# Lending part of an activations tile to a weight stream as four more raw tiles, and moving a scratch tile of the last block

## The chip, the cores and the metric

The kernel runs on one core of a Trainium2 chip, as one program in one launch. The metric is the device time of a run in microseconds (us). The engines are named as in the profile: PE (TensorE, matmuls; PEld its weight loads), DVE (VectorE), ACT (ScalarE), POOL (GpSimd) and SP (SyncE, which here only issues DMAs).

## The reference

Two models follow one another on 256 tokens of width 1024: a block of two layers (an mLSTM mixer in layer 0, latent attention in layer 1, each followed by a mixture of experts and a gated projection) and a second block (two feed-forward layers round a retention mixer). The change touches the mixture of experts, which both layers of the first block have:

```python
def peer_ffn(x, w_q, sub_keys, u, v):            # x: 256 x 1024
    q = (xt @ w_q).reshape(T, PEER_HEADS, 2, PEER_HALF)
    s = jnp.einsum('thcd,hcnd->thcn', q, sub_keys)
    s1, i1 = lax.top_k(s[:, :, 0], K)            # K = 16, of 128 keys
    s2, i2 = lax.top_k(s[:, :, 1], K)
    cand_s = s1[..., :, None] + s2[..., None, :] # 256 candidates
    top_s, top_pos = lax.top_k(cand_s, K)
    expert_idx = ...                             # 16 of 128*128 experts per head
    gates = jax.nn.softmax(top_s, axis=-1)
    act = gelu(einsum('thkd,td->thk', u[expert_idx], x))
    out = einsum('thk,thkd->td', gates * act, v[expert_idx])
```

## The kernel before

The kernel does not gather experts. It computes x times all of u (128 blocks of 128 experts), multiplies the activations with a gate matrix that is zero wherever an expert was not chosen, and multiplies the whole with v. One tile, `big`, holds the activations: 128 partitions by 128 blocks by 256 tokens, one block being 1 KB per partition; `room(big, n)` is the stretch of blocks 4n to 4n+3, as large as one weight unit.

**Precision and the stream.** A product in float32 is made from hi and lo parts: `split` (line 439) casts a value to a shorter form, hi (on ACT, line 440), and subtracts, lo (on DVE, or POOL for some units, line 441). All weights are units of 128 x 1024 and come through one `Stream` (`Net.w`). `load` (line 261) issues each unit's DMA on SP's queue into one of three tiles `wraw`. `prep` (line 281) makes hi and lo in one of three tiles each, `whi` and `wlo`, up to three units ahead of the unit PE is at (`target`). A raw tile is free again when its lo has been made, so `load_ahead` (line 314) keeps at most three units loaded or loading beyond those prepared.

**A stage of experts** (`peer`, line 878) takes 16 query units, 128 units of u, 128 units of v, in this order. `skew` runs query units, scores and the first blocks in a staggered way. `block(b)` (line 928) does 24 matmuls of 256 columns on one unit of u (`cols_late`, line 490): 16 with hi, then 8 with lo. Beside the blocks DVE makes the selection (`select`, line 1051), given out in portions of 1.8 us per block by `spend`, and this order of DVE's is fixed by hand (`in_order`); the order on the other engines is that of a scheduler. The selection lasts until about block 41. After it the class `Gates` makes the gate matrix in steps beside the remaining blocks.

**Every third block** does not burden DVE with its lo. For units in `on_dma`, `begin` (line 293) lets ACT write x = −raw (line 298) into one of two tiles x1, taken in turn, rounded to the short form, and a POOL DMA adds the raw unit onto it, which leaves raw less its rounded form, the lo part (line 299). The lo tile of such a unit is called x in the trace. `begin` is called when the unit is the next to be prepared and has been loaded; its hi follows from `prep` (line 287).

**The end of the blocks.** `activate` (line 1035) puts the gelu of a block into `big`; for tokens whose gates are there already it goes by a scratch tile: for even blocks `gl`, for odd blocks `gates.room`, the last 1 KB of x0, a tile of `Gates`. `joins` (line 1046) multiplies it in on DVE one block later. When all blocks are done, line 965 splits the first four blocks of `big` into W[0], whose hi takes the place of x0 and is named x in the trace (its lo is another x); the following groups go to a tile named xT. Then `rows_k` (line 547) multiplies them with the units of v into four accumulators.

Of the kernel before, what the change touches and what calls it, by code (L numbers as in the profile page):

```python
# [9 lines left out]
F32 = mybir.dt.float32  # L10
F32R = mybir.dt.float32r
# [8 lines left out]
P = 128  # L20
D = 1024
S = 256
# [11 lines left out]
UNIT = 1024  # L34
# [3 lines left out]
PLE_TAIL = 5  # L38
FF_TAIL = 6
PACE = 4  # L40

GATE_SCALE = 2.0 ** 15

# [176 lines left out]
class Ring:  # L220


    def __init__(self, size, new):
        self.size, self.new, self.units = size, new, []


class Stream:
# [3 lines left out]
    def __init__(self, k, pool, tag, size, widths, src, raw=3, parts=3):  # L231
        self.pool = pool
        self.k, self.tag, self.size, self.widths, self.src = k, tag, size, widths, src
        self.n, self.i, self.loaded, self.done, self.oldest = len(widths), 0, 0, 0, 0
        self.raw, self.ahead = raw, parts
        self.raws, self.parts = {}, {}
        self.on_pool, self.on_dma = set(), set()
        self.rings = [Ring(parts, lambda i: [self.tile(i, x, F32R, parts) for x in ("hi", "lo")])]
        self.start, self.until = 0, 0
        self.begun, self.spare = {}, None  # L240

    def tile(self, i, what, dt, bufs):
        return self.pool.tile([P, self.size], dt, tag=self.tag + what, name=f"{self.tag}{what}{i}", bufs=bufs)

    def extend(self, ring, until):

        self.rings = [self.rings[0], ring]
        self.start, self.until = self.i, until
        self.tail_at(until)

    def tail_at(self, i):

        self.on_pool.update(range(i, i + 2))

    def target(self):

        if self.i < self.until:
            return min(self.i + self.ahead + min((self.i - self.start) // PACE, self.rings[1].size), self.until + self.ahead)
        return self.i + self.ahead

    def load(self, i):
        t = self.tile(i, "raw", F32, self.raw)
        w = self.widths[i]
        self.k.nc.sync.dma_start(out=t[:, :w], in_=self.src[i, :, :w])
        self.raws[i] = t

# [14 lines left out]
    def prep(self, i, ring):  # L281
        k, w = self.k, self.widths[i]
        t = self.raws.pop(i)
        ring.units.append(i)
        if i in self.begun:
            hi, lo = self.tile(i, "hi", F32R, self.ahead), self.begun.pop(i)
            k.nc.scalar.copy(hi[:, :w], t[:, :w])
        else:
            hi, lo = ring.new(i)
            k.split(t[:, :w], hi[:, :w], lo[:, :w], pool=i in self.on_pool)  # L290
        self.parts[i] = (hi[:, :w], lo[:, :w])

# [9 lines left out]
    def fill(self):  # L302
        while self.done < min(self.n, self.target()):
            ring = self.ring(self.done)
            if ring is None:
                break
            self.load_ahead()
            self.prep(self.done, ring)
            self.done += 1
        self.load_ahead()  # L310
        if self.done in self.on_dma and self.done not in self.begun:
            self.begin(self.done)

    def load_ahead(self):
        while self.loaded < min(self.n, self.done + self.raw):
            self.load(self.loaded)
            self.loaded += 1

# [27 lines left out]
class Net:  # L346
# [44 lines left out]

    def more(self, pool, tail=TAIL, until=None):

        new = lambda i: [self.t(pool, [P, UNIT], f"more{x}", F32R, bufs=tail) for x in ("hi", "lo")]
        self.w.extend(Ring(tail, new), until or self.until)

    def in_order(self):
# [70 lines left out]
    def rstd(self, pool, var, n, eps, more=None):  # L468

        t = self.t(pool, [P, n], "rstd", bufs=4)  # L470
        if more is None:
            self.nc.vector.tensor_scalar_add(t, var, float(eps))
        else:
            self.nc.vector.tensor_scalar(t, var, more, float(eps), op0=ALU.add, op1=ALU.add)  # L474
        self.nc.gpsimd.tensor_tensor(t, t, self.mhalf[:, :n], op=ALU.pow)  # L475
        return t
# [401 lines left out]
    def peer(self, layer, gain):  # L878
        nc, v, tc = self.nc, self.nc.vector, self.tc
        mm = nc.tensor.matmul  # L880
        with tc.tile_pool(name="pr", bufs=1) as pool:
            big = self.t(pool, [P, P, S], "big")
# [16 lines left out]
            steps = self.select(tk, big, ready, idx, gT, iota)  # L899

            self.w.spare = lambda n: self.t(ip if n else self.gp, [P, UNIT], "x1", F32R)
            self.w.on_dma = set(range(self.w.i + 16 + 1, self.w.i + 16 + P - 8, 3))

            sc = self.scores_of(big)
# [57 lines left out]
            gates = now["gates"]  # L962
# [12 lines left out]
            n = P // WB  # L975
# [18 lines left out]
            parts = [(W[n - 1], j) for j in range(WB)]  # L994
# [40 lines left out]
    def activate(self, big, gates, late, b, ps):  # L1035

        nc = self.nc
        t0 = gates.tokens if gates else 0
        if t0:
            y = gates.room if b % 2 else self.t(gates.pool, [P, S], "gl")  # L1040
            nc.scalar.activation(y[:, :t0], ps[:, :t0], AF.Gelu)
            late.append((big[:, b, :t0], y[:, :t0]))
        if t0 < S:
            nc.scalar.activation(big[:, b, t0:], ps[:, t0:S], AF.Gelu)
# [467 lines left out]
    def neighborhood(self, pool, y, nqk, done):  # L1512
# [83 lines left out]
        for step in range(H8 + 4):  # L1596
            for s in (3, 2, 1):
                if 0 <= step - s < H8:
                    stages[s](step - s)
            next(more)  # L1600
            next(more)
            if step < H8:
                s_scores(step)
# [22 lines left out]
class Gates:  # L1626
# [42 lines left out]
    def join(self, g, blocks, done):  # L1669

        nc, TJ = self.k.nc, self.TJ
        t = slice(g * TJ, (g + 1) * TJ)
        ps = self.ps[g].rearrange("p (t b) -> p b t", t=TJ)
        dst = self.big[:, :blocks, t] if done else self.big[:, blocks:, t]
        if done and blocks:
            nc.vector.scalar_tensor_tensor(dst, ps[:, :blocks], 1.0 / GATE_SCALE, dst, op0=ALU.mult, op1=ALU.mult)
        if not done:
            if blocks < P:
                nc.scalar.mul(dst, ps[:, blocks:], 1.0 / GATE_SCALE)
            self.tokens = (g + 1) * TJ  # L1680
            self.ps.pop(g)
# [97 lines left out]
```

## Time and profile before

| | us |
|---|---|
| timed runs | 2660.10, 2676.08, 2676.26 (median 2676.08) |
| profiled execution, its own time | 2663.04 |
| span in the profile | 2661.3 |
| PE busy | 2559.8 (96%) |
| DVE busy | 1751.7 (66%) |
| ACT busy | 1328.9 (50%) |
| POOL busy | 244.5 (9%) |
| mean granted clock of TensorE | 0.988 |

In layer 0 the query units run from about 146 to 206 us of the span, the blocks from about 206 to 642, and the units of v from 647 on; in layer 1 the blocks run from about 1202 to 1640. Times in the trace are counted from the start of the span. A row such as "5.14 <-ACT x" in brackets says how long the engine was idle ahead of an instruction and what ended it. A granted clock of 1.00 is 2.4 GHz, 0.50 is 1.2 GHz.

### The profile page before, as it was taken

The page shows a single profiled execution, that of the slowest core. Times are in us where ns is not written, and L with a number is a line of the kernel's source. Part 1 is how long each engine was busy: PE and PEld are TensorE (multiplying, and loading weights), DVE is VectorE, ACT ScalarE, POOL GpSimd, SP SyncE. Part 2 cuts the span into 40 slices and gives each one's busy share as a digit, 9 for nine tenths or more (in the row PEclk, how much of TensorE's full clock was granted, in tenths as well). Part 3 has the DMA queues.
Part 4 walks back from the last instruction along what each step waited for, and adds up shares of the span by engine and source line. Part 5 has one row for each costly group of instructions (what it writes and reads, how often), then busy time and mean ns, then how long its engine had stood idle before and what let it go on. Part 6 is the DMA issues. An engine that isn't in the chain of part 4 may idle for free. (4 is left out here: it accounts for less than half of the span.)

```text
span 2661.3 us, 42846 instructions
## 1 busy us (share of the span) xinstructions
PE 2559.8 (96%) x16706; PEld 2308.8 (87%) x16706; DVE 1751.7 (66%) x3120; ACT 1328.9 (50%) x2113; POOL 244.5 (9%) x201
## 2 busy tenths in 40 slices
PE   8999899999999998999899999999999999999998
PEld 7799899998888887899889998888887997987898
DVE  6879856677555567689856677555557546665654
ACT  5445555554444445545545554444445444554542
POOL 0560000000000003000000000000001002111000
PEclk9999999999999999999999999999999999999999
DMA  7356677776555564357677776555565654554653
GB/s 249 108 168 196 197 209 202 207 207 207 199 195 194 191 211 160 119 170 199 196 205 200 213 203 209 200 195 191 195 208 188 223 167 152 183 177 157 204 194 101
DMA packets 144620, 502.42 MB, mean 189 GB/s; under 512 B 16153, under 2 KB 22425, under 8 KB 144417
## 3 DMA queue, kind: packets, MB, share of 16 engines
q1 hardware_dynamic: 122832, 443.93, 48.3%
q0 software_dynamic: 14032, 50.86, 10.3%
q10 hardware_dynamic: 7552, 4.89, 0.6%
q8 instruction: 131, 2.15, 0.3%
q14 instruction: 73, 0.59, 0.1%
HBM read 494.38 MB, written 5.24 MB: 188 GB/s over the span
## 5 line engine op out<-in xcount | busy, mean ns | idle before, releaser
L441 DVE TENSOR_TENSOR wlo<-wraw,whi 128x1024 fp32r<-128x1024 f32 (+1 forms) x478 | 587.3, 1229 | 531.9 <-ACT whi L440 531.1
L440 ACT CAST whi<-wraw 128x1024 fp32r<-128x1024 f32 x520 | 543.8, 1047 | 599.6 <-PE acc L547 322.8
L490 PE MATMUL ub<-xT,whi 128*128 128x256 f32 x4096 | 548.5, 287 | 4.3 <-ACT whi L440 3.5
L490 PEld LDWEIGHTS ub<-xT,whi 128*128 128x128 f32 x4096 | 515.8, 194 | 7.7 <-ACT whi L440 7.2
L547 PE MATMUL acc<-whi,xT 128*128 128x512 f32 x1816 | 507.5, 392 | 12.5 <-ACT whi L440 7.2
L547 PEld LDWEIGHTS acc<-whi,xT 128*128 128x128 f32 x1816 | 341.3, 189 | 85.8 <-ACT xT L440 7.6
L441 DVE TENSOR_TENSOR morelo<-wraw,morehi 128x1024 fp32r<-128x1024 f32 (+1 forms) x214 | 261.5, 1224 | 119.4 <-ACT morehi L440 118.9
L440 ACT CAST morehi<-wraw 128x1024 fp32r<-128x1024 f32 (+1 forms) x227 | 237.1, 1047 | 188.2 <-DMA wraw<-in_wst 72.9
L547 PE MATMUL acc<-wlo,xT 128*128 128x512 f32 x908 | 282.7, 391 | 0.2 <-DVE wlo L441 0.2
L547 PE MATMUL acc<-morehi,xT 128*128 128x512 f32 x808 | 235.1, 391 | 0.2
L547 PEld LDWEIGHTS acc<-wlo,xT 128*128 128x128 f32 x908 | 171.2, 189 | 37.0 <-DVE wlo L441 1.0
L490 PE MATMUL ub<-xT,wlo 128*128 128x256 f32 x1408 | 198.1, 283 | 1.9 <-DVE wlo L441 1.7
L441 POOL TENSOR_TENSOR wlo<-wraw,whi 128x1024 fp32r<-128x1024 f32 (+1 forms) x42 | 100.8, 2403 | 1047.8 <-ACT whi L440 1042.7
L490 PEld LDWEIGHTS ub<-xT,wlo 128*128 128x128 f32 x1408 | 181.6, 192 | 3.1 <-DVE wlo L441 3.1
L547 PEld LDWEIGHTS acc<-morehi,xT 128*128 128x128 f32 x808 | 151.8, 189 | 32.3 <-ACT morehi L440 0.6
L298 ACT ACTIVATE x<-wraw 128x1024 fp32r<-128x1024 f32 x80 | 84.7, 1058 | 152.6 <-DMA wraw<-in_wst 152.6
L446 PE MATMUL ps<-xT,whi 128*128 128x256 f32 (+1 forms) x552 | 158.6, 288 | 0.0
L447 PE MATMUL ps<-xT,whi 128*128 128x256 f32 (+1 forms) x552 | 156.9, 284 | 0.4 <-DVE xT L441 0.4
L448 PE MATMUL ps<-xT,wlo 128*128 128x256 f32 (+1 forms) x552 | 156.6, 284 | 0.0
L299 POOL DMA_DIRECT2D x<-in_wst x80 | 70.0, 875 | 798.6 <-ACT x L298 245.6
L547 PE MATMUL acc<-morelo,xT 128*128 128x512 f32 x404 | 129.1, 392 | 5.0 <-DVE morelo L441 5.0
L490 PE MATMUL ub<-xT,x 128*128 128x256 f32 x640 | 95.0, 292 | 34.7 <-DMA x<-in_wst 34.6
(477 smaller groups left out, 4132.4 us busy)
## 6 DMA issues: line engine op xcount, KB each, us to landing
wraw<-in_wst SPq DMA_DIRECT2D x816, 512.0 KB, 4.0
x<-in_wst POOLq DMA_DIRECT2D x80, 512.0 KB, 5.6
wraw<-in_wst SPq DMA_DIRECT2D x10, 384.0 KB, 3.4
sp<-x SPq DMA_DIRECT2D x4, 512.0 KB, 3.0
big<-in_keys ACTq DMA_DIRECT2D x8, 256.0 KB, 6.7
sp<-big SPq DMA_DIRECT2D x4, 512.0 KB, 4.3
x<-sp POOLq DMA_DIRECT2D x4, 512.0 KB, 4.7
pp<-sp SPq DMA_DIRECT2D x4, 512.0 KB, 5.6
```

Source lines behind the costliest of these rows:

```text
L298: k.nc.scalar.mul(lo[:, :w], self.raws[i][:, :w], -1.0)
L299: k.nc.gpsimd.dma_start(out=lo[:, :w], in_=self.src[i, :, :w], accum_op=ALU.add)
L440: self.nc.scalar.copy(hi, src)
L441: (self.nc.gpsimd if pool else self.nc.vector).tensor_tensor(lo, src, hi.bitcast(F32), op=ALU.subtract)
L446: mm(ps, a[0], b[0], start=start, stop=False)
L447: mm(ps, a[0], b[1], start=False, stop=False)
L448: mm(ps, a[1], b[0], start=False, stop=stop)
L490: mm(ps[:, :S], w[of][:, k], xT[part][:, k], start=n == 0, stop=n == len(steps) - 1)
L547: mm(acc[ti][h], a, w[b][:, h * 512:(h + 1) * 512], start=first, stop=last)
```

## The change

Rooms 14 to 17 of `big` (blocks 56 to 71) hold nothing until block 56. They are lent to the stream as four more raw tiles for the first 40 units of u (`SELECT`, `LENT`), so that in this stretch seven raw tiles go round. `load_ahead` loads up to seven units beyond those prepared while units are in this range. `begin` may be called for a unit up to two units earlier than before. hi and lo tiles are taken from their ring one by one. And the scratch tiles of `activate` are exchanged: even blocks take `gates.room`, odd blocks `gl`, so that the last block, 127, does not use x0's room. The assertion in `Gates.join` guards the rooms' use.

```diff
--- before.py
+++ after.py
@@ -38,6 +38,8 @@
 PLE_TAIL = 5
 FF_TAIL = 6
 PACE = 4
+
+SELECT, LENT = 40, 4
 
 GATE_SCALE = 2.0 ** 15
 
@@ -235,9 +237,10 @@
         self.raw, self.ahead = raw, parts
         self.raws, self.parts = {}, {}
         self.on_pool, self.on_dma = set(), set()
-        self.rings = [Ring(parts, lambda i: [self.tile(i, x, F32R, parts) for x in ("hi", "lo")])]
+        self.rings = [Ring(parts, lambda i, x: self.tile(i, x, F32R, parts))]
         self.start, self.until = 0, 0
         self.begun, self.spare = {}, None
+        self.lent_raws, self.borrow = [], range(0)
 
     def tile(self, i, what, dt, bufs):
         return self.pool.tile([P, self.size], dt, tag=self.tag + what, name=f"{self.tag}{what}{i}", bufs=bufs)
@@ -248,6 +251,10 @@
         self.start, self.until = self.i, until
         self.tail_at(until)
 
+    def lend(self, raws, units):
+
+        self.lent_raws, self.borrow = raws, units
+
     def tail_at(self, i):
 
         self.on_pool.update(range(i, i + 2))
@@ -259,8 +266,8 @@
         return self.i + self.ahead
 
     def load(self, i):
-        t = self.tile(i, "raw", F32, self.raw)
-        w = self.widths[i]
+        n, w = (i - self.borrow.start) % (self.raw + len(self.lent_raws)) - self.raw, self.widths[i]
+        t = self.lent_raws[n] if i in self.borrow and n >= 0 else self.tile(i, "raw", F32, self.raw)
         self.k.nc.sync.dma_start(out=t[:, :w], in_=self.src[i, :, :w])
         self.raws[i] = t
 
@@ -282,11 +289,12 @@
         k, w = self.k, self.widths[i]
         t = self.raws.pop(i)
         ring.units.append(i)
+        hi = ring.new(i, "hi")
         if i in self.begun:
-            hi, lo = self.tile(i, "hi", F32R, self.ahead), self.begun.pop(i)
+            lo = self.begun.pop(i)
             k.nc.scalar.copy(hi[:, :w], t[:, :w])
         else:
-            hi, lo = ring.new(i)
+            lo = ring.new(i, "lo")
             k.split(t[:, :w], hi[:, :w], lo[:, :w], pool=i in self.on_pool)
         self.parts[i] = (hi[:, :w], lo[:, :w])
 
@@ -308,11 +316,12 @@
             self.prep(self.done, ring)
             self.done += 1
         self.load_ahead()
-        if self.done in self.on_dma and self.done not in self.begun:
-            self.begin(self.done)
+        for i in range(self.done, self.done + (3 if self.done + 2 in self.borrow else 1)):
+            if i in self.on_dma and i not in self.begun:
+                self.begin(i)
 
     def load_ahead(self):
-        while self.loaded < min(self.n, self.done + self.raw):
+        while self.loaded < min(self.n, self.done + self.raw + (len(self.lent_raws) if self.loaded in self.borrow else 0)):
             self.load(self.loaded)
             self.loaded += 1
 
@@ -391,7 +400,7 @@
 
     def more(self, pool, tail=TAIL, until=None):
 
-        new = lambda i: [self.t(pool, [P, UNIT], f"more{x}", F32R, bufs=tail) for x in ("hi", "lo")]
+        new = lambda i, x: self.t(pool, [P, UNIT], f"more{x}", F32R, bufs=tail)
         self.w.extend(Ring(tail, new), until or self.until)
 
     def in_order(self):
@@ -899,6 +908,9 @@
             steps = self.select(tk, big, ready, idx, gT, iota)
 
             self.w.spare = lambda n: self.t(ip if n else self.gp, [P, UNIT], "x1", F32R)
+
+            first = self.w.i + 16
+            self.w.lend([self.room(big, n) for n in range(14, 14 + LENT)], range(first, first + SELECT))
             self.w.on_dma = set(range(self.w.i + 16 + 1, self.w.i + 16 + P - 8, 3))
 
             sc = self.scores_of(big)
@@ -1037,7 +1049,7 @@
         nc = self.nc
         t0 = gates.tokens if gates else 0
         if t0:
-            y = gates.room if b % 2 else self.t(gates.pool, [P, S], "gl")
+            y = self.t(gates.pool, [P, S], "gl") if b % 2 else gates.room
             nc.scalar.activation(y[:, :t0], ps[:, :t0], AF.Gelu)
             late.append((big[:, b, :t0], y[:, :t0]))
         if t0 < S:
@@ -1675,6 +1687,7 @@
         if done and blocks:
             nc.vector.scalar_tensor_tensor(dst, ps[:, :blocks], 1.0 / GATE_SCALE, dst, op0=ALU.mult, op1=ALU.mult)
         if not done:
+            assert self.k.w.done >= self.k.w.borrow.stop
             if blocks < P:
                 nc.scalar.mul(dst, ps[:, blocks:], 1.0 / GATE_SCALE)
             self.tokens = (g + 1) * TJ
```

On ACT, in the middle of layer 0's blocks with the selection, the rows before are these (`whi_…<-wraw` is the hi of a block's unit, `x_…<-wraw` the start of a third block's lo, and `big<-ub` the gelu of a finished block):

```order
L440 CAST whi_3275<-wraw_3156 128x1024
L1044 ACTIVATE big_1652<-ub_3233 128x256
L298 ACTIVATE x_386_3281<-wraw_3197 128x1024
L287 CAST whi_3319<-wraw_3197 128x1024
L1044 ACTIVATE big_1652<-ub_3274 128x256
L1044 ACTIVATE big_1652<-ub_3318 128x256
L440 CAST whi_3358<-wraw_3238 128x1024
```

And in the change, at the same block:

```order
L295 CAST whi_3189<-big_1652 128x1024
L306 ACTIVATE x_382_3192<-wraw_3030 128x1024
L1056 ACTIVATE big_1652<-ub_3149 128x256
L449 CAST whi_3230<-big_1652 128x1024
L1056 ACTIVATE big_1652<-ub_3188 128x256
L449 CAST whi_3270<-wraw_2991 128x1024
L1056 ACTIVATE big_1652<-ub_3229 128x256
L295 CAST whi_3311<-wraw_3030 128x1024
L306 ACTIVATE x_390_3315<-big_1652 128x1024
```

Before, x and whi of one unit (`wraw_3197`) stand side by side. In the change x_382 of the raw tile `wraw_3030` stands one triple ahead of the whi_3311 of the same tile, with the gelus of two blocks and two whi between them, and the raw tiles are partly rooms of `big`.

On POOL, in layer 0 ahead of the query units (`wlo` are lo parts of query units), before:

```order
L441 TENSOR_TENSOR wlo_1719<-wraw_1512,whi_1718 128x1024
L441 TENSOR_TENSOR wlo_1765<-wraw_1597,whi_1764 128x1024
L441 TENSOR_TENSOR wlo_1818<-wraw_1603,whi_1817 128x1024
L441 TENSOR_TENSOR wlo_1871<-wraw_1722,whi_1870 128x1024
L441 TENSOR_TENSOR wlo_1924<-wraw_1768,whi_1923 128x1024
L441 TENSOR_TENSOR wlo_1976<-wraw_1821,whi_1975 128x1024
```

and in the change:

```order
L450 TENSOR_TENSOR wlo_1719<-wraw_1512,whi_1718 128x1024
L450 TENSOR_TENSOR wlo_1765<-wraw_1597,whi_1764 128x1024
L307 DMA x_339_2447<-in_wst 128x1024
L450 TENSOR_TENSOR wlo_1818<-wraw_1603,whi_1817 128x1024
L450 TENSOR_TENSOR wlo_1871<-wraw_1722,whi_1870 128x1024
L450 TENSOR_TENSOR wlo_1924<-wraw_1768,whi_1923 128x1024
```

The first DMA into an x moved ahead of eleven of these wlo; on ACT its negation moved with it. On SP the loads of the four lent rooms stand among and behind the spills of `peer` (line 1003), ahead of most of the loads of query units.

On ACT at the end of layer 0's blocks (`gl` and `x_319` are the scratch tiles, `x_683` is the hi of W[0], `xT` that of W[1], `morehi` a further unit of v), before:

```order
L1041 ACTIVATE gl_7994<-ub_7927 128x256
L440 CAST whi_8016<-wraw_7895 128x1024
L440 CAST morehi_8034<-wraw_7932 128x1024
L1041 ACTIVATE x_319_2180<-ub_7962 128x256
L440 CAST xT_8013<-big_1652 128x1024 x2
L440 CAST x_683_7997<-big_1652 128x1024
```

and in the change:

```order
L1053 ACTIVATE x_319_2180<-ub_7905 128x256
L449 CAST whi_7995<-wraw_7874 128x1024
L449 CAST x_683_7975<-big_1652 128x1024
L1053 ACTIVATE gl_7980<-ub_7941 128x256
L449 CAST xT_7992<-big_1652 128x1024 x2
L449 CAST morehi_8013<-wraw_7910 128x1024
```

x_683 moved ahead of the last gelu, of the two casts to xT and of morehi.

On DVE at the same place (`big<-gl` and `big<-x_319` are the joins, x_684 is the lo of W[0]), before:

```order
L1049 TENSOR_TENSOR big_1652<-x_319_2180,big_1652 128x256
L1049 TENSOR_TENSOR big_1652<-gl_7994,big_1652 128x256
L441 TENSOR_TENSOR wlo_8017<-wraw_7895,whi_8016 128x1024
L441 TENSOR_TENSOR morelo_8035<-wraw_7932,morehi_8034 128x1024
L1049 TENSOR_TENSOR big_1652<-x_319_2180,big_1652 128x256
L441 TENSOR_TENSOR xT_8013<-big_1652,xT_8013 128x1024 x2
L441 TENSOR_TENSOR x_684_7998<-big_1652,x_683_7997 128x1024
```

and in the change:

```order
L1061 TENSOR_TENSOR big_1652<-gl_7939,big_1652 128x256
L1061 TENSOR_TENSOR big_1652<-x_319_2180,big_1652 128x256
L450 TENSOR_TENSOR wlo_7996<-wraw_7874,whi_7995 128x1024
L450 TENSOR_TENSOR x_684_7976<-big_1652,x_683_7975 128x1024
L1061 TENSOR_TENSOR big_1652<-gl_7980,big_1652 128x256
L450 TENSOR_TENSOR xT_7992<-big_1652,xT_7992 128x1024 x2
L450 TENSOR_TENSOR morelo_8014<-wraw_7910,morehi_8013 128x1024
```

x_684 moved ahead of the last join, of xT and of morelo. The order of DVE and of PE within the blocks is the same as before but for names.

## Rows read from the trace of the kernel before

**Rows 1.** The page's costliest groups (busy us, mean ns of one | idle us before).

```profile
L298 ACT ACTIVATE x<-wraw 128x1024 fp32r<-128x1024 f32 x80 | 84.7, 1058 | 152.6 <-DMA wraw<-in_wst 152.6
...
L299 POOL DMA_DIRECT2D x<-in_wst x80 | 70.0, 875 | 798.6 <-ACT x L298 245.6
...
L490 PE MATMUL ub<-xT,x 128*128 128x256 f32 x640 | 95.0, 292 | 34.7 <-DMA x<-in_wst 34.6
```

**Rows 2.** Windows: PE, PEld, DVE, ACT, POOL busy us (instructions), granted clock, DMA share, GB/s.

```profile
206.00:294.00 88.00, 80.05 (x631) 78.51 (x630) 83.02 (x316) 41.43 (x60) 7.05 (x8) 0.96 0.69 196
294.00:348.50 54.50, 46.24 (x348) 44.84 (x348) 42.03 (x79) 31.96 (x46) 4.38 (x5) 0.94 0.70 202
642.30:656.00 13.70, 8.55 (x28) 6.50 (x28) 7.42 (x7) 5.83 (x8) 0.59 (x2) 0.75 0.48 189
1202.00:1301.00 99.00, 88.50 (x704) 86.30 (x703) 93.24 (x351) 46.60 (x68) 7.76 (x9) 0.98 0.69 197
1301.00:1343.00 42.00, 35.87 (x274) 35.45 (x273) 32.09 (x45) 26.52 (x38) 3.46 (x4) 0.92 0.68 195
1640.40:1654.00 13.60, 8.90 (x32) 6.63 (x32) 7.63 (x8) 6.34 (x8) 0.64 (x2) 0.87 0.61 203
```

**Rows 3.** DVE's waits in 207 to 293, 293 to 350 and 1300 to 1350.

```profile
DVE q L441 <- ACT q L440: 1.1, 1, 1.1
...
DVE wlo L441 <- ACT whi L440: 10.6, 6, 4.1
...
DVE wlo L441 <- ACT whi L440: 11.4, 7, 4.2
```

**Rows 4.** Waits of ACT and of SP's queue in 206 to 346.

```profile
ACT whi L440 <- DMA wraw<-in_wst: 32.8, 13, 6.0
...
SPq L264 <- DVE wlo L441: 51.5, 15, 6.3
```

**Rows 5.** PE's timeline in layer 0 (start, us, work), blocks 34 to 41.

```profile
331.55 2.08 PE L490 MATMUL ub<-xT,whi 128*128 128x256 f32 x16
...
334.43 2.08 PE L490 MATMUL ub<-xT,whi 128*128 128x256 f32 x16
...
351.36 0.49 PE L1114 MATMUL ps<-ident,big 128*128 128x128 f32 x3
351.60 0.61 PE L490 MATMUL ub<-xT,whi 128*128 128x256 f32 x3
```

**Rows 6.** PE's timeline: lo of block 27 in both layers, blocks 41 and 43 in layer 1.

```profile
300.25 1.22 PE L490 MATMUL ub<-xT,wlo 128*128 128x256 f32 x8
...
1295.04 1.21 PE L490 MATMUL ub<-xT,wlo 128*128 128x256 f32 x8 [0.20 <-DVE wlo L441]
...
1346.17 2.16 PE L490 MATMUL ub<-xT,whi 128*128 128x256 f32 x16
...
1356.21 1.22 PE L490 MATMUL ub<-xT,x 128*128 128x256 f32 x8 [2.12 <-DMA x<-in_wst]
```

**Rows 7.** Line 299, 206 to 349: issue on POOL (ns, count), and landing.

```profile
L299 POOL DMA_DIRECT2D x<-in_wst x13: 876/876/906, 210.5 to 341.7; - x13
...
DMA to landing us min/median/max: 5.3/7.1/8.4
```

**Rows 8.** POOL's timeline in layer 0's query units; ten rows like this one.

```profile
164.53 2.41 POOL L441 TENSOR_TENSOR wlo<-wraw,whi 128x1024 fp32r<-128x1024 f32 x1 [1.12 <-ACT whi L440]
```

**Rows 9.** ACT's timeline at the seam of layer 0.

```profile
641.38 1.05 ACT L440 CAST whi<-wraw 128x1024 fp32r<-128x1024 f32 x1 [1.28 <-PE ub L490]
...
646.35 1.04 ACT L440 CAST x<-big 128x1024 fp32r<-128x1024 f32 x1
```

**Rows 10.** PE at the seams of both layers: timeline, then a window of the tile acc.

```profile
647.45 1.22 PE L547 MATMUL acc<-whi,x 128*128 128x512 f32 x2 [5.14 <-ACT x L440]
...
1644.70 0.76 PE L547 MATMUL acc<-whi,x 128*128 128x512 f32 x2 [4.23 <-ACT x L440]
...
647.40:652.00 4.60, 4.55 (x10) 0.50 0.76 305
```

## The prediction

> **What bounds the kernel now.** I began with the page's costliest groups. TensorE (PE) is busy for 2559.8 of 2661.3 us, so only about 100 us can be won without taking work away, and the question is which idle stretches the change can reach. One group names a single cause: the matmuls that read the tile x (the lo part of every third block, which comes by ScalarE and a GpSimd DMA) stand idle for 34.7 us ahead of themselves, 34.6 of it until that DMA lands [rows 1].
>
> Then the busy time by stage [rows 2]. Where selection and blocks run together the loss differs from stretch to stretch: in 206 to 294 (layer 0) PE is busy for 80.05 of 88 us and VectorE (DVE) for 83.02; in 294 to 348.5 PE for 46.24 of 54.5 but DVE for only 42.03. Layer 1 has the same two phases: DVE 93.24 of 99.00 us, then 32.09 of 42. And at the seam from the blocks to the V units PE works 8.55 of 13.7 us (642.3 to 656) and 8.90 of 13.6 (1640.4 to 1654).
>
> DVE's waits tell the phases apart. In the first phase it waits for nothing but 1.1 us; in the second it waits 10.6 us in six stops in layer 0 and 11.4 in seven in layer 1, each time for ScalarE's (ACT) whi [rows 3]. So the first phase is DVE's: PE waits there for x, but it could not run ahead of the lo parts that DVE makes between steps of the selection. The second is a chain of waits round the raw tiles: ACT's whi waits 32.8 us in 13 stops for a raw tile to land, and the load on SP's queue stood 51.5 us in 15 stops behind DVE's wlo, the last reader of one of only three raw tiles [rows 4].
>
> **Selection, phase 1: nothing.** Seven raw tiles instead of three, and an x begun two units earlier, end PE's waits for x (about 7 of the 88 us). But DVE's order there is written by hand and is the same row for row, with nothing to wait for. PE's idle time moves from x to wlo. Value: 0 us. Bounds: 0, and what PE stood idle there, 88 − 80.05 = 7.95 in layer 0 and 99 − 88.50 = 10.5 in layer 1, if DVE were not the bound after all.
>
> **Selection, phase 2.** A block that waits for nothing takes 334.43 − 331.55 = 2.88 us (24 matmuls) [rows 5]. The lo matmuls of block 27 begin at 300.25 in layer 0 and at 1295.04 in layer 1 [rows 6]; I take these as set by DVE, since they close its phase. From there to the first matmul of block 41 stand 0.96 us (2.88/3, eight matmuls), 13 blocks of 2.88 = 37.44, and two groups of three transposes at 351.60 − 351.36 = 0.24, 0.5 together [rows 5]: 38.9. To this I add 1.5 for lo parts that DVE still brings late: its own work in the whole of 294 to 348.5 is 42.03 us, nearly PE's for the same blocks, so it follows closely but hardly falls behind (ends: 0, and 42.03 − 38.9 = 3.1 if DVE's work is the bound). So 40.4 us: block 41 begins at 340.7 instead of 351.60 (−10.9) and at 1335.4 instead of 1346.17 (−10.7) [rows 5, 6]. In layer 1 block 43 also waits 2.12 us for x, begun late for the same want of a raw tile [rows 6]: −2.1. Sum −23.7.
>
> Is x then early enough? In the new order ACT begins x(i+3) right behind whi(i), a whole triple of blocks ahead. Its tile comes free when PE has done block i−3, and PE wants it at the lo of block i+3: five blocks and the 16 hi matmuls of a sixth, 5 × 2.88 + 1.92 = 16.3 us. The chain is the negation, 1.06 us, the DMA's issue, 0.88, and its landing, at most 8.4 [rows 1, 7]: 10.3. There are 6 us to spare.
>
> The Trainium skill ("SBUF — State Buffer", SBUF: two separate sides) speaks against this: a DMA issued from GpSimd has its descriptors written there, and VectorE's two-port operations lock GpSimd out, so that such a DMA waits for VectorE; a denser VectorE would make x later still. By its example (about 3100 ns for 620) 2.5 us would be added and the sum would stay. Without it: the issue took 876 to 906 ns in all 13 cases between 206 and 349, with DVE at 94% in most of it [rows 2, 7], but the landing, 5.3 to 8.4 us, does spread, and I keep a later landing as a rival.
>
> **Hoisted work.** The first x of a lent tile is begun before most query units: one negation on ACT and one issue on POOL, ahead of eleven wlo that POOL makes for the query units. POOL does one in 2.41 us and then stands idle 1.12 until the next whi (ten such rows) [rows 8], so an issue of 0.9 us goes into one such gap. Value 0; 1 us per layer if it does not. SP's four early loads go past spills that nobody waits for soon: 0. The number of loads and bytes is unchanged, so are DVE's and PE's rows within the blocks.
>
> **The seam to V.** Before, ACT did whi (641.38), morehi, the last gelu, two casts to xT, and only then x, the hi of W[0], at 646.35; it could not be sooner, since the last block's gelu stood in x's room. PE stood idle 5.14 us until 647.45 [rows 9, 10]. Now x stands right behind whi. whi ends at 642.43, x at 643.48, and its lo is made behind it on DVE, after four matmuls of cover. PE last worked until 647.45 − 5.14 = 642.31, so idle is 1.2, and I add 0.3 for the lo: 1.5, a gain of 3.6. In layer 1 the idle is 4.23 [rows 10]; the same 1.5 leaves a gain of 2.7. Then the clock: after the idle stretch PE worked 647.4 to 652 at a granted 0.50 (the 1.2 GHz level), 4.55 us for what takes 2.28 at full rate [rows 10]. After the idle of 2.12 us at 1356.21, by contrast, eight matmuls took 1.22 us [rows 6], where at half clock they would take over 2 × 0.96 = 1.92; so an idle of 1.5 leaves the clock up, −2.3; in layer 1 the window's mean clock is 0.87 where layer 0's is 0.75 [rows 2], so by 0.13/0.25 about half, −1.2. Sum −9.8. Bounds: −6.3 if the clock falls all the same; 0 if x waits for something else.
>
> **Sum.** −23.7 − 9.8 = −33.5 us against the profiled execution: 2663.0 − 33.5 = 2629.5. The three timed runs and the profiled one lie at 2660.1, 2663.0, 2676.1 and 2676.3; from their middle, 2669.6, the same sum gives 2636. Between the two I say **2633 us**.
>
> **Rivals.**
> 1. *Only the seam gains* (0.13). DVE stays the bound through phase 2 as well: what it waited for before is filled by other waits of its hand-written order (the transposes and gT at the end of each half of the selection hang on PE and ACT). For it: DVE's 42.03 us are nearly PE's work. Against it: the six stops all name whi. −9.8: 2653 to 2660.
> 2. *Half of phase 2* (0.12). x lands late although it begins sooner, since seven loads in flight share the DMA engines with it and DVE is denser. Past the 6 us to spare each x stops PE again. −12 − 9.8: about 2645.
> 3. *Slower* (0.05). ACT works in order. x(i+3) now stands ahead of the gelu of block i−3 and of whi(i+1), and it waits for its raw tile and for PE to leave its own tile. Each raw load that lands late then holds up the hi parts too, which x did not before. PE has three prepared units, 3 × 2.88 = 8.6 us, less whi's 1.05 and x's 1.06 themselves: it decides from a wait of 6.5 us on. There are 2 × 13 such x; to eat the 33.5 and add 1%, 27 us, each would have to wait 6.5 + 60/26 = 8.8 us. Against it: the lent tiles are loaded seven units ahead. About 2695.
> 4. *It does not do what it says* (0.03): the lent rooms come free too late to hold loads, and all stays within 1%, 2655 to 2669.
> 5. *More* (0.10): phase 1 gains too, up to 7.95 + 10.5 of PE's idle: about 2618.
>
> **Chances and range.** The forecast itself holds 0.57: 2622 to 2645, from 0 to 3.1 us of late lo parts per layer, the clock's 3.5, and the two levels of the runs. A measurement tells about 1% from no change, here 27 us from 2676 or 2663, so a gain under 27 would be called no change: the forecast against a run of the same level is −33.5, near that bound. Faster by over 1%: 0.57 less the part in which 6 us are lost (0.09), and rivals 5 and a part of 2: 0.48 + 0.10 + 0.04 = 0.62; within 1%: 0.33; slower 0.05. For the range I take 2614, from rival 5 with the lower level, to 2657, from rival 1's lower end: it leaves out rivals 3 and 4, half of 1, and little else.
>
> **What would show it.** In phase 1 the matmuls of x no longer wait for the DMA, and those of wlo do for DVE, with DVE's waits still near nothing. The loads no longer wait for DVE's wlo, nor whi for the raw tile. From block 27 to 41 some 40 us instead of 51. x lands in 5 to 9 us but well ahead of PE. At the seams an idle of 1 to 2 us and a granted clock near 1. I am wrong if PE's idle time in phase 2 stays with another name, if ACT's x or whi waits for a raw tile for more than 6 us, or if DVE's phase 1 itself grows longer.

## The result and the profile after

| | before | after |
|---|---|---|
| median of the runs, us | 2674.40 | 2641.97 |
| runs, us | 2660.10 to 2676.26 | 2641.24 to 2642.56 |
| profiled execution, its own time, us | 2663.04 | 2641.24 |
| span of the profile, us | 2661.3 | 2639.5 |

The ratio is 0.9892, with a 95% interval of 0.9862 to 0.9922: faster by about 1.1%, 2642 us where 2633 was forecast. The kernel before has medians between 2661 and 2674 us in different series of runs, so each ratio below is against the kernel before in the same series. The two profiled executions are 21.8 us apart, and the forecast made for them was 33.5. Read off PE's matmuls in both traces, stretch by stretch:

| stretch | before, us | after, us | difference |
|---|---|---|---|
| start to block 0, layer 0 | 206.5 | 211.9 | +5.5 |
| blocks 0 to 27, layer 0 | 94.8 | 93.6 | −1.2 |
| blocks 28 to 40 | 50.3 | 38.8 | −11.5 |
| blocks 41 to 127 | 290.7 | 289.9 | −0.8 |
| idle at the seam to V | 5.14 | 1.13 | −4.0 |
| V, latent attention, query units of layer 1 | 555.0 | 561.2 | +6.2 |
| blocks 0 to 27, layer 1 | 93.6 | 93.6 | 0.0 |
| blocks 28 to 40 | 50.1 | 38.7 | −11.4 |
| blocks 41 to 127 | 294.3 | 290.8 | −3.5 |
| idle at the seam to V | 4.23 | 1.13 | −3.1 |
| from there to the end | 1016.6 | 1018.7 | +2.1 |

So the gains are where they were forecast and of about that size, and two stretches got longer: those that hold the query units. The windows of the change, in the columns of [rows 2], for the same stretches:

```profile
211.90:304.50 92.60, 83.83 (x672) 80.98 (x671) 87.65 (x333) 48.55 (x68) 7.87 (x9) 1.00 0.73 204
304.50:344.30 39.80, 39.52 (x326) 39.20 (x327) 37.83 (x63) 28.38 (x40) 3.49 (x4) 1.00 0.70 177
634.20:648.00 13.80, 12.67 (x55) 10.25 (x55) 9.77 (x10) 8.41 (x10) 2.17 (x4) 1.00 0.76 263
1196.50:1289.10 92.60, 83.88 (x673) 81.04 (x672) 87.78 (x334) 48.50 (x68) 7.74 (x9) 1.00 0.73 206
1289.10:1328.90 39.80, 39.54 (x327) 39.21 (x327) 37.80 (x63) 28.52 (x41) 3.46 (x4) 1.00 0.71 178
1619.60:1633.00 13.40, 12.27 (x53) 9.87 (x53) 9.69 (x9) 8.12 (x10) 2.01 (x4) 1.00 0.78 269
```

In the first and fourth row (blocks 0 to 27) DVE is busy for 87.65 and 87.78 of 92.6 us and PE for 83.83 and 83.88: phase 1 is DVE's as before. In the second and fifth (blocks 27 to 40) PE is busy for 39.52 and 39.54 of 39.8 us, where in [rows 2] it had 46.24 of 54.5. A part of this gain is the clock: [rows 2] have a granted 0.94 and 0.92 there, the change 1.00, which by the length of those two stretches is an estimated 3.3 us in each layer. The third and sixth rows are the seams: 12.67 of 13.8 and 12.27 of 13.4 us, and the granted clock is 1.00 instead of 0.75 and 0.87.

The page has one group that answers to the x of [rows 1]; x itself waits no longer and has left the list:

```profile
L499 PE MATMUL ub<-xT,wlo 128*128 128x256 f32 x1408 | 201.5, 286 | 18.0 <-DVE wlo L450 18.0
```

PE now stands 18.0 us for DVE's wlo. PE's waits in blocks 0 to 27 and 27 to 40 of layer 0 say where:

```profile
PE ub L499 <- DVE wlo L450: 8.0, 13, 0.9
...
PE ub L499 <- DVE wlo L450: 1.0, 2, 0.7
```

8.0 us in 13 stops in phase 1, 1.0 in phase 2. The waits of ACT and of SP's queue from 212 to 344, beside [rows 4]:

```profile
ACT x L306 <- DMA wraw<-in_wst: 4.4, 4, 1.5
ACT x L306 <- DMA big<-in_wst: 3.5, 3, 2.3
...
SPq L271 <- DVE wlo L450: 69.6, 18, 6.3
```

ACT's whi does not wait for a raw tile any more (32.8 us before); only x does, for 7.9 us in seven stops, the longest of 2.3 us, and none of them stops PE. SP's loads still wait for DVE's wlo, 69.6 us, longer than before, although the prediction had them wait no longer: with seven tiles they are that far ahead, and the wait reaches nobody.

The lo of block 27 and block 41, as in [rows 5, 6]:

```profile
304.51 1.21 PE L499 MATMUL ub<-xT,wlo 128*128 128x256 f32 x8 [0.74 <-DVE wlo L450]
...
344.07 0.49 PE L1126 MATMUL ps<-ident,big 128*128 128x128 f32 x3
344.31 1.92 PE L499 MATMUL ub<-xT,whi 128*128 128x256 f32 x14
```

From 304.51 to 344.31 are 39.8 us. Forecast were 40.4, and in the kernel before it was 51.35.

The issue and landing of x on POOL's queue, as in [rows 7]:

```profile
L307 POOL DMA_DIRECT2D x<-in_wst x14: 873/873/902, 205.5 to 340.9; - x14
...
DMA to landing us min/median/max: 5.3/6.8/9.0
```

The issue takes 873 to 902 ns with DVE at 95% in phase 1 (87.65 of 92.6 us). The Trainium skill ("SBUF — State Buffer", SBUF: two separate sides) states that a DMA issued from GpSimd has to wait while VectorE runs a two-port operation. Such a wait does not show here: the issue got no longer, the landing (5.3 to 9.0 us) only at its upper end by 0.6. No run here tells which of VectorE's operations in this stretch are of that kind.

ACT and PE at the seams, as in [rows 9, 10]: ACT in layer 0, PE in layers 0 and 1, and the window of acc behind the first.

```profile
633.29 1.05 ACT L449 CAST whi<-wraw 128x1024 fp32r<-128x1024 f32 x1 [1.48 <-PE ub L499]
634.24 1.04 ACT L449 CAST x<-big 128x1024 fp32r<-128x1024 f32 x1
...
635.34 0.73 PE L556 MATMUL acc<-whi,x 128*128 128x512 f32 x2 [1.13 <-ACT x L449]
...
1620.78 0.73 PE L556 MATMUL acc<-whi,x 128*128 128x512 f32 x2 [1.13 <-ACT x L449]
...
635.30:640.00 4.70, 4.66 (x20) 1.00 0.62 211
```

x stands right behind whi (633.29, 634.24), the idle is 1.13 us in both layers, and the clock stays at 1.00. Compared matmul by matmul the first seam brings 6.2 us (PE is ahead by 8.1 us before it and by 14.3 after it), the second 5.1.

Now what was not forecast. PE falls back by 6.3 us between 151 and 181 us of the trace of before, and by 9.4 between 1157 and 1186: at the head of the query units of both layers. SP's queue in layer 0, the change:

```profile
148.74 0.39 SPq L271 DMA_DIRECT2D big<-in_wst  x1
150.48 1.30 SPq L1015 DMA_DIRECT2D sp<-big  x2
154.28 1.11 SPq L271 DMA_DIRECT2D big<-in_wst  x2
```

Three loads of 512 KB into rooms of `big` go out between 148.74 and 155.4, among the spills. Just then ACT's queue issues the loads of the keys and, at 151.51, of iota (64 KB): one lent load goes out ahead of iota's, two within 4 us behind it. In layer 1 it is one ahead (1130.22) and three within 6 us behind (from 1135.48; iota 1132.97). In the kernel before, SP's next load goes out 5.7 us (158.21) and 4.4 us (1152.86) behind iota's. iota's landing in the change (min, median, max of the two layers):

```profile
DMA to landing us min/median/max: 11.4/13.2/15.1
```

and in the kernel before:

```profile
DMA to landing us min/median/max: 6.4/6.4/6.4
```

ACT waits for it, since the cast of iota (line 1654) stands among the first rows of the query units (layer 0, and the same row of layer 1):

```profile
162.93 0.40 ACT L1654 CAST x<-iota 128x256 f16<-128x256 f32 x1 [4.53 <-DMA iota<-in_iota]
163.24 1.05 ACT L306 ACTIVATE x<-big 128x1024 fp32r<-128x1024 f32 x1
...
1148.11 0.40 ACT L1654 CAST x<-iota 128x256 f16<-128x256 f32 x1 [8.51 <-DMA iota<-in_iota]
```

4.53 and 8.51 us, in which all that is behind it on ACT stands: the hoisted x, whi, and the q of the query units. In the kernel before ACT waited 1.4 us there in both layers together. PE's waits in the query units follow:

```profile
PE ps L455 <- ACT q L449: 2.8, 1, 2.8
...
PE ps L455 <- ACT q L449: 6.6, 1, 6.6
```

2.8 us in layer 0 and 6.6 in layer 1; before, PE waited there for 0.2 us and nothing. Behind the 2.8 us PE works at the lower clock level (1.2 GHz) for a while, as a window of this stretch shows by its granted clock of 0.50; behind the 6.6 us the mean granted clock is 0.60 over 8 us:

```profile
166.50:169.70 3.20, 3.20 (x17) 3.20 (x17) 3.20 (x1) 1.15 (x4) 3.20 (x2) 0.50 1.00 164
1150.00:1158.00 8.00, 7.27 (x40) 7.27 (x41) 5.62 (x19) 3.88 (x10) 0.91 (x1) 0.60 0.63 149
```

### The profile page after: what moved, and what is told of

Same layout as the page of the kernel before. It is cut to its first block, busy times and chain, and to the rows that moved or that the text cites. A ratio compares the mean times of both kernels' runs of the same rounds, so it can differ in the third digit from the quotient of the medians.

```text
span 2639.5 us, 42830 instructions
## 1 busy us (share of the span) xinstructions
PE 2552.9 (97%) x16706; PEld 2303.4 (87%) x16706; DVE 1751.2 (66%) x3120; ACT 1331.9 (50%) x2113; POOL 245.2 (9%) x201
## 3 DMA queue, kind: packets, MB, share of 16 engines
q0 software_dynamic: 14032, 50.86, 10.5%
## 5 line engine op out<-in xcount | busy, mean ns | idle before, releaser
L450 DVE TENSOR_TENSOR wlo<-wraw,whi 128x1024 fp32r<-128x1024 f32 x448 | 549.6, 1228 | 501.5 <-ACT whi L449 500.5
L449 ACT CAST whi<-wraw 128x1024 fp32r<-128x1024 f32 (+1 forms) x490 | 512.3, 1047 | 511.0 <-PE acc L556 304.2
L499 PE MATMUL ub<-xT,whi 128*128 128x256 f32 x4096 | 540.8, 285 | 4.8 <-ACT whi L449 4.4
L499 PEld LDWEIGHTS ub<-xT,whi 128*128 128x128 f32 x4096 | 508.9, 191 | 7.1 <-ACT whi L449 6.8
L306 ACT ACTIVATE x<-wraw 128x1024 fp32r<-128x1024 f32 x66 | 69.9, 1060 | 139.1 <-DMA wraw<-in_wst 139.1
L457 PE MATMUL ps<-xT,morelo 128*128 128x256 f32 x416 | 117.7, 283 | 0.0
## 6 DMA issues: line engine op xcount, KB each, us to landing
big<-in_keys ACTq DMA_DIRECT2D x8, 256.0 KB, 11.3
```

What stands on the lines that cost most here:

```text
L306: k.nc.scalar.mul(lo[:, :w], self.raws[i][:, :w], -1.0)
L449: self.nc.scalar.copy(hi, src)
L450: (self.nc.gpsimd if pool else self.nc.vector).tensor_tensor(lo, src, hi.bitcast(F32), op=ALU.subtract)
L457: mm(ps, a[1], b[0], start=False, stop=stop)
L499: mm(ps[:, :S], w[of][:, k], xT[part][:, k], start=n == 0, stop=n == len(steps) - 1)
```

## The experiments

Each kernel differs from the change, where nothing else is said, by the edit shown. Its name stands in brackets. "PE falls back" and "is ahead" are by the starts of the same matmuls in this kernel's trace and in that of the kernel before.

**The two parts apart.** First only the scratch tiles' exchange (swap_only):

```diff
-SELECT, LENT = 40, 4
+SELECT, LENT = 0, 0
```

> Only the exchange of the scratch tiles, no lent rooms. If the seams' share of the gain (6.2 us at the first, 5.1 at the second, read off the two traces) is the exchange's own, the span is about 2661.3 - 11 = 2650 us, block 0 of layer 0 begins at 206.5 as before, PE still waits for x about 32 us in the selections, and the idle at the seams is below 2 us. If the seams gained from the lending instead, the span stays near 2661.

Ratio 0.9952 (0.9933 to 0.9970), span 2650.8 us. PE's waits at the first seam and in layer 0's selection:

```profile
PE acc L556 <- ACT x L449: 1.1, 1, 1.1
...
PE ub L499 <- DMA x<-in_wst: 15.8, 9, 2.8
```

The seam has its 1.1 us without any lent tile, and x keeps PE waiting 15.8 us in layer 0's selection and 15.4 in layer 1's. Matmul by matmul the seams bring 6.2 and 5.1 us, as in the change: the exchange brings its 11.3 us alone.

Then only the lending (lend_only):

```diff
-            y = self.t(gates.pool, [P, S], "gl") if b % 2 else gates.room
+            y = gates.room if b % 2 else self.t(gates.pool, [P, S], "gl")
```

> The lent rooms with the scratch tiles as before. If the two parts add up, span about 2639.5 + 11 = 2651 us: the selections gain 26 us, the query units lose 16 (block 0 of layer 0 at 212 instead of 206.5), the seams' idle is 5.1 and 4.2 us. If they depend on one another, it is nearer 2640 or 2661.

Ratio 0.9938 (0.9912 to 0.9963), median 2648.9 us. The blocks 28 to 40 take 38.8 and 38.7 us, block 0 begins at 210.2, and without the exchange both seams wait on:

```profile
PE acc L556 <- ACT x L449: 4.2, 1, 4.2
```

0.0048 and 0.0062 of gain make 0.0110, the whole has 0.0108: within their intervals of 0.002 to 0.003 the parts add up. The profiled execution, 2640.7 us of span, came out 10 us under what was expected. Of this its blocks 41 to 127 have 5.5 us (286.8 and 288.4 instead of 289.9 and 290.8); that stretch is the same in both kernels and goes between 286 and 295 us from execution to execution, so a single span is not the measure of a part. Medians and stretches are.

**What the query units lose.** The loads into lent rooms kept behind what is written ahead of them on SP's queue (loads_in_order):

```diff
-        self.k.nc.sync.dma_start(out=t[:, :w], in_=self.src[i, :, :w])
+        d = self.k.nc.sync.dma_start(out=t[:, :w], in_=self.src[i, :, :w])
+        if i in self.borrow and n >= 0:
+            self.k.tc.keep_in_program_order(d)
```

> The change, but the loads into lent rooms stay behind the loads written ahead of them on SP's queue instead of going to the stage's start. If they cause the loss ahead of the query units (theory A: they hold up the 64 KB load of iota, ACT waits for it; theory B: the first x, begun as soon as its lent room is full, takes ACT's and POOL's time), block 0 begins at 206 again, the span is about 2639.5 - 15.7 = 2624 us, and the selections keep their 26 us. If the loss has another cause, the span stays near 2640.

Ratio 0.9847 (0.9813 to 0.9881), median 2624.69, span 2623.2 us. Block 0 begins at 205.9 us, and at the head of the query units PE falls back by nothing in either layer: the 15.7 us are back. But blocks 0 to 27 take 94.9 and 98.5 us instead of 93.6 and 93.6. That the span is as expected to 1 us is luck: these 6.2 us are lost, and about as much is won in stretches that the edit does not touch, 5.2 us of it in the blocks 41 to 127. The landing of iota, then ACT and DVE among layer 1's first blocks:

```profile
DMA to landing us min/median/max: 6.4/6.5/6.6
...
1181.72 1.06 ACT L308 ACTIVATE x<-big 128x1024 fp32r<-128x1024 f32 x1 [5.72 <-DMA big<-in_wst]
...
1184.01 0.42 DVE L452 TENSOR_TENSOR q<-ps,q 128x256 fp32r<-128x256 f32 x1 [5.71 <-ACT q L451]
```

iota lands in 6.4 to 6.6 us again. The second row is the price: now the lent room is late, x stands 5.72 us on ACT for it, the q behind it is late, and DVE (third row) stands 5.71 us for that q, in the phase that DVE sets. It is the mechanism of the rival on the slow side.

Then the early loads as in the change, with only the cast of iota kept behind the work written ahead of it (iota_in_order):

```diff
-        k.nc.scalar.copy(self.iota, iota.unsqueeze(2).to_broadcast([P, P, 2]))
+        k.tc.keep_in_program_order(k.nc.scalar.copy(self.iota, iota.unsqueeze(2).to_broadcast([P, P, 2])))
```

> The change, with the early loads and the early x where they are, but ACT's cast of iota behind the work written ahead of it, eight query units later. Theory A (iota lands late and ACT waits at its cast): the wait of 4.5 us in layer 0 and 8.5 in layer 1 goes, block 0 at about 207, span about 2625 to 2630. Theory B (the early x itself, 1.05 us on ACT and 0.9 on POOL): nothing changes, block 0 at 212, span 2640.

Ratio 0.9862 (0.9828 to 0.9896), span 2622.6 us. In layer 1 theory A holds: at the head of the query units PE falls back by 1.8 us instead of 9.4. In layer 0 it does not hold alone: PE falls back by 4.4 us instead of 6.3, and block 0 begins at 210.9. ACT, POOL, DVE and PE's wait there:

```profile
160.98 1.06 ACT L306 ACTIVATE x<-big 128x1024 fp32r<-128x1024 f32 x1 [2.45 <-DMA big<-in_wst]
...
162.66 1.06 POOL L307 DMA_DIRECT2D x<-in_wst  x1 [0.88 <-DMA big<-in_keys]
163.44 7.41 POOL L450 TENSOR_TENSOR wlo<-wraw,whi 128x1024 fp32r<-128x1024 f32 x3
...
163.62 5.02 DVE L450 TENSOR_TENSOR klo<-big,khi 128x128 fp32r<-128x128 f32 x1
...
172.70 0.27 DVE L450 TENSOR_TENSOR klo<-big,khi 128x128 fp32r<-128x128 f32 x1
...
PE ps L457 <- DVE q L450: 2.4, 1, 2.4
```

x has taken iota's place: it stands 2.45 us for its lent room, the hi parts behind it are late, and on POOL the DMA issue and three wlo follow each other without a gap (the idle of 1.12 us of [rows 8] is gone). The delay reaches PE by way of DVE. The lo of 128 keys (klo) takes DVE 0.27 us while POOL stands idle (fifth row), but 5.02 us here: it ends at 168.64, about 0.15 us behind the end of the second of the three wlo. In the kernel before, where POOL pauses between its wlo, the klo of the query units that meet one also end about 0.15 us behind it and take at most 2.05 us. DVE's q behind the klo is late, and PE stands 2.4 us for it. The change itself has the same klo of 5.02 us. So in layer 0 the early loads and the early x lose 4.4 us without iota's help; in layer 1, where POOL makes no lo of query units, all but 1.8 us of the loss is iota's.

The four first lent loads at the eighth query unit, by hand, on top of the loads in their written place (loads_at_query_7). The edit is cut; `early` calls `load` for the first four lent units:

```diff
             def s_query(hc):
+                if hc == 7:
+                    self.w.early()
```

> The four first lent loads issued at the eighth query unit, pinned there: after iota, ahead of the blocks. With the loads in their written place ACT waited 5.7 us in layer 1 for a lent room ahead of the blocks and VectorE with it. If that wait is what made phase 1 of layer 1 longer (98.5 us from block 0 to 28 instead of 93.6), it goes, span 2618 to 2620 against 2623.2. If VectorE's chain alone sets the end of phase 1, both begin block 28 at the same time and the span stays at 2623.

Ratio 0.9852 (0.9820 to 0.9884), span 2632.5 us beside a median of 2671.9 for the kernel before. DVE waits for nothing in blocks 0 to 27 of layer 1, which take 93.6 us again. From the head of layer 1's query units to block 28 PE falls back by 0.7 us, with the loads in order by 4.9: the 4 us that were hoped for are there. From V's first matmul to block 28 it is 649.0 us against 649.7 all the same, since V and the latent attention, which this edit does not touch, took 3.5 us longer in this execution. The ratio, with its interval of 0.0032 (some 8 us), can't tell such a gain.

**Tiles or the earlier begin.** The lent tiles with begin for the next unit only (begin_late):

```diff
-        for i in range(self.done, self.done + (3 if self.done + 2 in self.borrow else 1)):
+        for i in range(self.done, self.done + 1):
```

> The change, but begin is called for the next unit only, as before: the lent raw tiles are there, x starts a triple later. If the raw tiles are what phase 2 lacked, PE's waits for x fall below 5 us in the two selections and the span stays near 2640 us. If the earlier begin is what counts (10.3 us of chain against 3 blocks of 8.64 and 1.92 of hi matmuls), x is wanted about when it lands: waits for x of 5 to 15 us in all, the selections gain about half, span 2645 to 2655.

Ratio 0.9890 (0.9858 to 0.9923), as the whole change. Blocks 28 to 40 take 38.7 us in both layers. PE's waits in layer 0's selection, then ACT's rows in it (L295 is the hi of a third block's unit, L306 the start of its lo), and two of the same rows in the change:

```profile
PE ub L499 <- DVE wlo L450: 9.1, 15, 0.9
...
277.59 1.05 ACT L295 CAST whi<-wraw 128x1024 fp32r<-128x1024 f32 x1 [1.59 <-PE ub L499]
...
279.77 1.06 ACT L306 ACTIVATE x<-big 128x1024 fp32r<-128x1024 f32 x1 [0.85 <-DMA big<-in_wst]
...
288.04 1.05 ACT L295 CAST whi<-big 128x1024 fp32r<-128x1024 f32 x1 [1.59 <-PE ub L499]
...
278.15 1.06 ACT L306 ACTIVATE x<-big 128x1024 fp32r<-128x1024 f32 x1 [0.74 <-DMA big<-in_wst]
...
286.83 1.05 ACT L295 CAST whi<-big 128x1024 fp32r<-128x1024 f32 x1 [1.59 <-PE ub L499]
```

No wait for x is left. But x does not begin a triple later in this kernel: it stands 8.3 us ahead of the whi of its own unit (279.77 and 288.04), in the change 8.7 (278.15 and 286.83), in the kernel before about 1. The edit moves the call of begin; the order of ACT's rows is the scheduler's, and in it x only stands behind one gelu more. So the written-out earlier begin is not needed, but this run does not take the early x away. How much the raw tiles do by themselves and how much the early x adds stays open: no run here has lent tiles and a late x. The span, 2645.7, is that of a series in which the kernel before was slower too.

**Is phase 1 DVE's?** Less of the selection beside each block, with the loads in order (spread_15):

```diff
-                elif spend(steps, 1.8):
+                elif spend(steps, 1.5):
```

> The loads in their written place, and 1.5 us of the selection beside each block instead of 1.8. If VectorE bounds phase 1 (28 blocks in 93.6 us where PE alone needs 80.6), a sixth less of the selection per block brings VectorE under PE: 28 blocks in about 84 us, the selection lasts to about block 49, and the span falls by 12 to 20 us to 2605 to 2611. If something else held PE there, the time from block 0 to 28 stays above 90 us and the span at 2623 or above.

Ratio 0.9782 (0.9753 to 0.9811), 0.0065 better than with the loads in order alone. Blocks 0 to 27 take 85.4 and 87.0 us instead of 94.9 and 98.5: DVE set them. The span, 2612.7 us, is 10.5 below that with the loads in order, less than the 12 to 20 expected: the blocks 41 to 127 take 290.3 and 294.5 us instead of 286.4 and 289.1.

The change once more, to lie beside the last two (change_again):

> The changed kernel itself once more, to lie beside the next two on one chip. The ratio to the kernel before should be 0.989 again, block 0 of layer 0 at 212 us, and ACT's wait for iota 4.5 us in layer 0 and 8.5 in layer 1; if that wait were chance, it would differ by more than 1 us.

Ratio 0.9917 (0.9897 to 0.9936), a little less than at first; the intervals overlap. Block 0 begins at 211.3 us, and ACT waits 4.7 and 9.7 us for iota. The second wait is 1.2 us longer than at first, more than the 1 us set above, but both are there again at the same place: that they occur is not chance. By this ratio the gain is 0.8%, so whether it is more or less than 1% stays open.

And further, again on top of the loads in order, with lent tiles for more blocks, since the selection then lasts longer (spread_13):

```diff
-SELECT, LENT = 40, 4
+SELECT, LENT = 48, 4
-                elif spend(steps, 1.8):
+                elif spend(steps, 1.3):
```

> Lent loads in their written place, 1.3 us of the selection beside each block, 48 units with lent tiles. With 1.5 us the 28 blocks of phase 1 took 85.4 and 87.0 us, where PE alone needs 80.6, and some blocks still stood 0.3 to 0.8 us for VectorE. If VectorE's load per block sets that, 28 blocks take 82 to 83 us, and the span falls by 4 to 8 us below spread_15's 0.978 of the kernel before (about 0.976). If the gates, now with fewer blocks to stand beside (from block 57 on), make VectorE late there, that is lost again between block 57 and 127, and the ratio is 0.978 or above.

Ratio 0.9726 (0.9707 to 0.9745), median 2586.94 us, better than expected and the fastest kernel here. Windows of blocks 0 to 28 and 28 to 127 of layer 0, columns as above:

```profile
206.00:290.00 84.00, 82.86 (x690) 82.51 (x690) 76.42 (x273) 50.40 (x72) 8.78 (x10) 1.00 0.90 255
290.00:609.00 319.00, 318.55 (x2908) 316.85 (x2907) 244.43 (x445) 183.69 (x371) 25.41 (x29) 1.00 0.71 207
```

PE is busy for 82.86 of 84 and 318.55 of 319 us: on layer 0's blocks there is hardly anything left to win but PE's own work. In layer 1 blocks 0 to 27 take 85.1 us. The gates have fewer blocks to stand beside and still fit in.

The same spreading in the kernel before (spread_before):

```diff
-                elif spend(steps, 1.8):
+                elif spend(steps, 1.5):
```

> The kernel before with 1.5 us of selection per block and nothing else. If only VectorE bounds phase 1 there, it gains 8 us per layer like the changed kernel, ratio 0.994. If the raw tiles bound it as soon as VectorE doesn't (x waits 7 to 9 us per layer in phase 1 and more with every block), the blocks with selection get nothing or little faster, ratio 0.998 to 1.004.

Ratio 0.9965 (0.9952 to 0.9978): a gain, about 9 us by the ratio, between the two that were expected. Blocks 0 to 27 take 91.4 and 89.7 us. PE's waits in layer 0's:

```profile
PE ub L490 <- ACT whi L440: 6.6, 6, 1.8
```

PE now waits for hi parts, 6.6 us, where the kernel before has no such wait; on ACT, x stands 45.2 us there for raw units to land. With three raw tiles the loads hold up phase 1 as soon as DVE doesn't: it stays at 91.4 and 89.7 us, with the lent tiles it comes to 85.4 and 87.0. Blocks 28 to 40 win too, 44.1 and 44.6 us instead of 50.3 and 50.1. Whether tiles and spreading bring more together than each alone stays open: by the ratios the spreading is worth 0.0065 with the tiles and 0.0035 without, with intervals of about 0.005 and 0.001; by blocks 0 to 127 of both layers in the profiled executions it is 11.0 us with them and 15.0 without.

## Why the prediction was right, and where it was off

- **Phase 1, nothing.** Right. 94.8 and 93.6 us became 93.6 and 93.6, and PE's idle moved from x to wlo, 8.0 us in each layer. spread_15 shows the cause and not only the place.
- **Phase 2, −23.7 us.** Right: −11.5, −11.4 and the wait of 2.1 us that block 43 of layer 1 lost are −25.0. The chain of waits round the raw tiles went as forecast: ACT's whi waits for no raw tile any more (32.8 us before), DVE's wlo waits for no whi. x is early, as forecast: in the change it lands 4.8 us or more ahead of PE's first matmul with it (6 us were forecast to be spare), which leaves rival 2 out. Which of the two, tiles or early x, the gain needs was not separated: begin_late did not make x late.
- **The seam, −9.8 us.** Right in kind, a little small: the idle fell to 1.13 where 1.5 was taken, the clock brought 2.2 and 2.0 us where 2.3 and 1.2 were taken, and the whole is −11.3. swap_only shows it alone.
- **Hoisted work, 0 us.** This is the term that failed: it measured +15.7 (6.3 and 9.4). I priced ACT's negation and POOL's issue, and passed over "SP's four early loads" with the remark that they go past spills that nobody waits for soon. What they delay is not on SP's queue at all: while ACT's queue fetches keys and iota, three of them (layer 0) or four (layer 1) are under way, iota lands in 11.4 and 15.1 us instead of 6.4, and a cast near the head of ACT's order waits for it. loads_in_order gives the time back. Nor did the gap of 1.12 us on POOL of [rows 8] cover the early x in layer 0: iota_in_order shows that POOL, once late, works without gaps, that DVE's klo then lasts 5.02 us, and that PE waits for the q behind it.
- **The rival on the slow side** (x holds up ACT while it waits for a raw tile) cost time in the blocks once, with 5.72 us in loads_in_order, below the 6.5 us from which it was to decide: it came among the first blocks of layer 1, in DVE's phase, and DVE stood 5.71 us behind it.
- **The number.** 33.5 us less 15.7 is 17.8; the profiled executions are 21.8 apart. The rest: 1.5 more at the seams, 1.3 in phase 2, 1.2 in phase 1 of layer 0, 2.2 in the blocks 41 to 127 beside block 43 and 1.8 in the stages ahead of the query units, against 4.1 lost in the later stages, which the change does not touch. Of these 4.1 I show no cause; from the second seam to the end the kernels here take from 1013.2 to 1019.1 us. The forecast of 2633 was below the measured 2642 for this reason: a loss of 15.7 that stood in the sum as 0. That 2642 still lies within the forecast's 2622 to 2645 is in part luck, since the small gains of this list were not forecast; 2633 with the 15.7 would have been 2649.

## What to carry to other kernels

A buffer that is free early may be filled early by the scheduler, as it was here: look for what else moves in those microseconds on the other DMA queues, and for the small load that an engine working in order waits for. Before more buffers are lent to a stage, ask which engine sets its pace: here the tiles paid only in the phase that was not VectorE's. And undo the parts of a change one by one, but check in the trace that the part is really gone: the earlier begin was taken out of the program, and x still began as early.

## What the runs showed that I had not expected

A load of 64 KB landed in 11.4 and 15.1 us instead of 6.4 when one load of 512 KB was issued shortly ahead of it and two or three shortly behind it, on another queue. Which of them held it up is not shown. A subtraction of 128 x 128 on VectorE took 0.27 us beside an idle GpSimd and 5.02 us beside two subtractions of 128 x 1024 that followed each other there without a gap. And PE's clock after an idle stretch: behind 2.78 us of waiting in layer 0's query units the matmuls went at the lower level for about 3 us, behind 1.13 us at the seams never, so that to a wait of 2.8 us an estimated 1.6 more came (half of the window of 3.20 us at 0.50). In layer 1 the wait is 6.6 us, and PE falls back by 9.4.
